# Memory attention: output products of the second token half run between the first half's scores, with their weights loaded once per half

## The chip, the cores and the metric

One Trainium2 chip; the program runs on one of its cores. The metric is the device time of one execution in microseconds (us), lower is better. The kernel before takes 2602.53 us, the median of 3 runs (2601.81 to 2604.06).

## The reference

One layer of a hybrid decoder for 512 prompt tokens and 32 sample tokens (8 sequences of 4), width 2048, everything in float32. Cut to what matters here:

```python
x = x + token_mixer(rmsnorm(x, norm_mix_w), ...)
# memory cross-attention: 4 heads of 128, 256 memory rows
q = rmsnorm(x) @ w_mq
s = einsum('blhd,bmhd->bhlm', q, mem_k) * 128 ** -0.5
o = einsum('bhlm,bmhd->blhd', softmax(s), mem_v)
x = x + o.reshape(B, L, 512) @ w_mo          # 512 x 2048
x = x + (silu(h @ w_gate) * (h @ w_up)) @ w_down   # h = rmsnorm(x)
```

Prompt tokens share one memory, whose keys and values were made earlier in the program; each sample sequence has a key and a value cache of its own (`cache_mem_k`, `cache_mem_v`, 512 KB per sequence each).

## The kernel before

Activations lie transposed: a tile holds 128 of the 2048 channels on its partitions and all 544 tokens along its free dimension. `X` is the residual, 16 such tiles in four groups. Float32 products are made of split operands: each operand is a rounded high part and a low part (`hi`, `lo`), and a product is three matmuls, high by high, high by low, low by high. For a weight, `load_part` (L117 to L134) loads 512 KB into `wraw`, ScalarE (ACT) casts it to `whi` (L131), VectorE (DVE) subtracts (`wlo`, L132). Three `wraw` buffers and two pairs of parts exist; the parts are made one ahead of their use (`parts_ahead`).

Work of TensorE (PE) that can fill gaps is put into a queue `line` of generators; `draw(n)` takes n matmuls (or small groups) from its head. The tile framework then orders the instructions of each engine by its own estimate of times, so the order in the program is not quite that of the source; each engine executes its order strictly.

The stage of this case lies between the mixer's output products and the SwiGLU:

- Eight query products (`add_mq`, 16 weight tiles of 3 matmuls each): four heads for tokens 256 to 543 (half 1), then four heads for tokens 0 to 255 (half 0).
- Between them, per head and half: scores (`x_scores`, `xs_ps`), a softmax on DVE and ACT, the turn of the probabilities on PE (`x_turn`, `xt_ps`), the products with the values (`x_values`, `xo_ps`), and the split of the result into `oxh` and `oxl` (`put_ox`).
- The samples' attention (`xsample`) in pieces: 16 pieces that turn keys and score them (`xk_ps`, `xss_ps`), a softmax, then eight pieces with the values (`xso_ps`). The 16 cache loads pass through three buffers (`xkv`), issued by SyncE's queue (SP), which executes its rows in order. `x_more` draws one piece. Half 1 of `ox` is complete only when the samples are done.
- The output products with `w_mo` (`add_mo(i, half)`, L1534 to L1567): for each of eight pairs of channel tiles (i) and each half of 272 tokens, 24 matmuls into `mo_ps`, of which there are two buffers. Then DVE adds the result to `X` (`x`, L1556), ACT squares it, and the squares are added up for the next norm, for half 0 on GpSimd (POOL, `SS`) and for half 1 on DVE (`SW`), both L1562. The weights of an i are loaded once and used for both halves.
- When both halves of an i are in `X`, `ffn_parts` (L1576 to L1595) makes operands of the SwiGLU's seven products (a Winograd scheme over halves of tokens and of channels): `B11` and `B21` from tokens 0 to 271 alone (ACT the high parts, DVE the low parts, L1583), and `b12`, `b22`, `t1`, `t2`, `t4` from both halves: ACT, DVE (`t`, L1534), POOL (`t`, L1589), DVE (`f`, L1534). The split of `t1` and `t2` into `T1` and `T2` (L606, L607) follows one i later. The SwiGLU's units (`unit`) use `B11`, `B21`, `T2`, `T1`, ... in this order; POOL combines weights for them (`scomb`, L1661) and operands (L1799).

The order of the output products is half 0 of i = 0 and 1 beside the last scores, then half 1 of i = 0 and 1, then for i = 2 to 7 half 1 and half 0.

Of the kernel before, what the change touches and what calls it, by code (L numbers as in the profile page):

```python
# [25 lines left out]
TT = TP + TS  # L26
# [18 lines left out]
def hybrid_step(ctx: ExitStack, tc: tile.TileContext, a):  # L45
    nc = tc.nc
    dma = nc.sync.dma_start
    dma2 = nc.gpsimd.dma_start
# [11 lines left out]
    dpool = pool("dpool", space=DRAM)  # L60
# [6 lines left out]
    def acc_tile(name):  # L67
        return ps_acc.tile([P, 2, 512], F32, tag="acc", name=name)
# [241 lines left out]
    line = deque()  # L310
# [3 lines left out]
    def parts_ahead(late=None):  # L314

        before = []
        for i in count():
            if i == late:
                yield from before
                before = []  # L320
            if not wants:
                break
            w, n0, k0, n, width = wants.popleft()
            now = [(k0 + j, *p) for j, p in enumerate(load_part(w, k0, n, n0, width))]
            yield from before
            before = now
        yield from before
# [295 lines left out]
    def xt(k):  # L623
        return X[k // 4][:, k % 4, :]
# [858 lines left out]
    def x_values(h, half):  # L1483
# [18 lines left out]

    for n, u in enumerate(units):
        need(("mq", *u))
        if n:
            x_turn(*units[n - 1])
            draw(4)
        else:
            draw(36)
        x_scores(*u)  # L1510
        draw(14)
        if n:
            x_values(*units[n - 1])
        for _ in range(6 if n >= MH - 1 else 0):
            x_more(1)
            draw(5)
    def ops_tiles(p, tag, name):
        return group(p, tag, name, F32R, (P, KH, HT))

    x3_d = dpool.tile([P, KD, TT], F32, name="x3_d")  # L1520
    h_d = dpool.tile([P, FF // P, TT], F32, name="h_d")
    fops = {}

    def x_ops(n, q):
        fops[q] = [ops_tiles(xnp, f"x{c}{n}", q + c) for c in "hl"]

    x_ops(0, "B11")
    x_ops(1, "B21")

    def ffn_w(out, o, t):  # L1530
        nc.scalar.activation(out, xt(o)[:, t], AF.Copy, scale=vcol("ffn", o))

    def ffn_w_less(out, o, t, y):
        nc.vector.scalar_tensor_tensor(out, xt(o)[:, t], vcol("ffn", o), y, ALU.mult, SPLIT)  # L1534

    S3 = [post.tile([P, 2, HT], F32, tag=t, name=t) for t in ("SS", "SW")]

    def add_mo(i, half, done=None):


        def run():
            if i not in mo_w:
                mo_w[i] = [next(wparts) for _ in range(MH)]
            acc = acc_tile("mo_ps")
            for k, hi, lo in mo_w[i]:
                xh, xl = ox[half][k]
                for u in range(2):
                    s = slice(u * P, (u + 1) * P)
                    for wt, xt_, at in ((hi, xh, 0), (hi, xl, 1), (lo, xh, 2)):
                        nc.tensor.matmul(  # L1550
                            acc[:, u, :HT], wt[:, s], xt_,
                            start=k + at == 0, stop=k == MH - 1 and at == 2,
                        )
                        yield
            x = X[i // 2][:, 2 * i % 4 : 2 * i % 4 + 2, (T0, T1)[half]]
            nc.vector.tensor_tensor(x, x, acc[:, :, :HT], ALU.add)  # L1556
            if i == 0:
                nc.scalar.activation(S3[half], x, AF.Square)
            else:
                t = post.tile([P, 2, HT], F32, tag="sqt", name="sqt", bufs=2)  # L1560
                nc.scalar.activation(t, x, AF.Square)
                (nc.vector if half else nc.gpsimd).tensor_add(S3[half], S3[half], t)  # L1562
            if done:
                done(i)

        line.append(run())


    mo_w, late, before = {}, [], []

    def t_parts(i, ts):
        for q, t in zip(("T1", "T2"), ts):
            split(*(t[:, i] for t in fops[q]), t)

    def ffn_parts(i):
        b12, b22, t4 = (t[:, i] for t in late)  # L1576
        ffn_w(b12, 2 * i, T1)
        ffn_w(b22, 2 * i + 1, T1)
        for u, q in enumerate(("B11", "B21")):
            o = 2 * i + u  # L1580
            hi, lo = (t[:, i] for t in fops[q])
            ffn_w(hi, o, T0)
            nc.vector.scalar_tensor_tensor(  # L1583
                lo, xt(o)[:, T0], vcol("ffn", o), hi.bitcast(F32), ALU.mult, SPLIT
            )
        t1 = ap.tile([P, HT], F32, tag="t1", name="t1", bufs=2)
        t2 = ap.tile([P, HT], F32, tag="t2", name="t2")
        ffn_w_less(t1, 2 * i, T0, b12)
        nc.gpsimd.tensor_tensor(t2, b22, t1, ALU.add)  # L1589
        ffn_w_less(t4, 2 * i + 1, T0, t2)  # L1590
        if before:
            t_parts(*before.pop())
        before.append((i, (t1, t2)))
        if i % 2:
            dma2(x3_d[:, 2 * i - 2 : 2 * i + 2], X[i // 2])  # L1595
# [516 lines left out]
```

## Time and profile before

| | |
|---|---|
| median of 3 runs | 2602.53 us |
| profiled execution | 2602.59 us, of it the span of its instructions 2600.8 us |
| PE busy | 2522.0 us, 97% of the span |
| DVE, ACT, POOL busy | 1687.6, 1583.4, 1079.2 us |
| query products (L1444) | 975.4 to 1063.0 us from the span's start |
| output products (L1550) | 1063.6 to 1133.0 us |

A row of the timeline names the engine, the line, the operation, output and inputs. Matmuls are pipelined: a row's own time (0.29 us) is longer than the distance to the next.

### The profile page before, as it was taken

Reading aid. Unit: us, or ns where it says so; the run is one execution under the profiler, and the core shown is the slowest. Engines: PE = TensorE matmul, PEld = TensorE weight load, DVE = VectorE, ACT = ScalarE, POOL = GpSimd, SP = SyncE. Lnnn points to the kernel's source line nnn. Section 1 sums busy time; section 2 is a strip of 40 time slices with the busy share of each in tenths; the row PEclk is TensorE's granted clock in tenths of the full one; section 3 lists DMA queues with packets and bytes.
Section 4 is the critical chain, followed back from the end, with each engine's and each line's share of the span. In section 5 each row is a group of like instructions: output and inputs, shape, how many; then the busy total and the mean of one; then the engine's idle time right before and its main releaser. Section 6 shows DMA issues by size and latency. Waiting matters only on the chain.

```text
span 2600.8 us, 48404 instructions
## 1 busy us (share of the span) xinstructions
PE 2522.0 (97%) x19679; PEld 2453.4 (94%) x19679; DVE 1687.6 (65%) x2575; ACT 1583.4 (61%) x2177; POOL 1079.2 (41%) x616
## 2 busy tenths in 40 slices
PE   8999999999999999989999999999999999999997
PEld 7999999998999998879999999999999999999997
DVE  5555555556568795697665656565666666767897
ACT  5343222333326785467777777777777778777757
POOL 4101222112124631255555555555555656665622
PEclk9999999999999999999999999999999999999999
DMA  7222332454523326522333333333333453333325
GB/s 236 83 69 82 91 91 91 143 155 137 179 66 128 106 72 192 193 100 96 123 114 111 115 106 115 106 115 106 115 107 120 158 187 132 115 115 135 112 70 162
DMA packets 287168, 315.48 MB, mean 121 GB/s; under 512 B 9508, under 2 KB 239220, under 8 KB 284097
## 3 DMA queue, kind: packets, MB, share of 16 engines
q1 hardware_dynamic: 273024, 264.80, 32.0%
q0 software_dynamic: 13920, 47.58, 5.5%
q8 instruction: 155, 2.54, 0.4%
q14 instruction: 69, 0.56, 0.1%
HBM read 278.28 MB, written 33.64 MB: 120 GB/s over the span
## 4 chain that ended last, share of the span: by engine, by line
PE 83%; DVE 7%; ACT 4%; issue 2%; DMA 2%; POOL 1%; SPq 0%; ACTq 0%; POOLq 0%; DVEq 0%
PE s_ps L1696 49%; PE in_ps L345 18%; PE o_ps L1149 4%; PE ha_ps L933 2%; PE d_ps L154 1%; DVE wlo L132 1%; PE mq_ps L1444 1%; PE o_ps L509 1%; PE s_ps L471 1%; DMA wraw<-in_w_in_dram 1%; DVE slo L1644 1%; PE mkv_ps L684 1%; PE in_ps L154 1%; DMA wraw<-in_w_down_dram 1%; PE t_ps L489 0%
## 5 line engine op out<-in xcount | busy, mean ns | idle before, releaser
L1644 DVE TENSOR_TENSOR slo<-scomb,h 128x1024 fp32r<-128x1024 f32 x256 | 311.5, 1217 | 132.3 <-PE s_ps L1696 113.9
L131 ACT CAST whi<-wraw 128x1024 fp32r<-128x1024 f32 (+1 forms) x204 | 169.7, 846 | 351.8 <-PE in_ps L345 278.0
L1642 ACT CAST h<-scomb 128x1024 fp32r<-128x1024 f32 x256 | 260.9, 1019 | 132.0 <-DVE slo L1644 118.7
L1661 POOL TENSOR_TENSOR scomb<-sraw 128x1024 f32<-128x1024 f32 x128 | 315.8, 2467 | 9.4 <-DVE slo L1644 4.4
L1643 ACT CAST shi<-scomb 128x1024 fp32r<-128x1024 f32 x256 | 269.7, 1053 | 53.0 <-PE s_ps L1696 49.5
L1661 POOL TENSOR_TENSOR scomb<-sraw,scomb 128x1024 f32<-128x1024 f32 x64 | 166.7, 2605 | 287.4 <-DVE slo L1644 241.6
L345 PE MATMUL in_ps<-xh,whi 128*128 128x272 f32 x1280 | 276.9, 297 | 0.8 <-ACT whi L131 0.8
L345 PE MATMUL in_ps<-xl,whi 128*128 128x272 f32 x1280 | 275.1, 295 | 0.0
L345 PE MATMUL in_ps<-xh,wlo 128*128 128x272 f32 x1280 | 272.9, 294 | 0.8 <-DVE wlo L132 0.8
L132 DVE TENSOR_TENSOR wlo<-wraw,whi 128x1024 fp32r<-128x1024 f32 (+1 forms) x204 | 208.3, 1034 | 98.8 <-ACT whi L131 94.8
L1696 PE MATMUL s_ps<-T,shi 128*128 128x272 f32 x1408 | 269.3, 288 | 2.8 <-ACT shi L1643 2.8
L1642 ACT CAST h<-sraw 128x1024 fp32r<-128x1024 f32 x192 | 195.3, 1017 | 122.3 <-DVE slo L1644 121.9
L611 DVE TENSOR_TENSOR gu<-gu,s_ps 128x272 f32<-128x272 f32 x264 | 111.6, 437 | 237.4 <-PE s_ps L1696 237.4
L1696 PE MATMUL s_ps<-dT,shi 128*128 128x272 f32 x1280 | 243.8, 289 | 0.0
L1644 DVE TENSOR_TENSOR slo<-sraw,h 128x1024 fp32r<-128x1024 f32 x192 | 233.2, 1215 | 10.7 <-ACT h L1642 7.3
L1643 ACT CAST shi<-sraw 128x1024 fp32r<-128x1024 f32 x192 | 201.5, 1049 | 56.5 <-PE s_ps L1696 48.0
L1696 PEld LDWEIGHTS s_ps<-T,shi 128*128 128x128 f32 x1408 | 221.2, 188 | 3.3 <-ACT shi L1643 3.0
L345 PEld LDWEIGHTS in_ps<-xh,wlo 128*128 128x128 f32 x1280 | 202.6, 189 | 6.4 <-issue 4.4
L345 PEld LDWEIGHTS in_ps<-xh,whi 128*128 128x128 f32 x1280 | 202.2, 189 | 6.7 <-issue 4.3
L345 PEld LDWEIGHTS in_ps<-xl,whi 128*128 128x128 f32 x1280 | 202.5, 189 | 5.1 <-issue 4.4
L1696 PE MATMUL s_ps<-T,slo 128*128 128x272 f32 x704 | 203.6, 289 | 1.2 <-DVE slo L1644 1.2
L1696 PEld LDWEIGHTS s_ps<-dT,shi 128*128 128x128 f32 x1280 | 201.1, 188 | 0.0
(521 smaller groups left out, 7371.6 us busy)
## 6 DMA issues: line engine op xcount, KB each, us to landing
sraw<-in_w_gate_dram SPq DMA_DIRECT2D x44, 1024.0 KB, 5.3
sraw<-in_w_up_dram SPq DMA_DIRECT2D x44, 1024.0 KB, 5.3
wraw<-in_w_in_dram SPq DMA_DIRECT2D x84, 512.0 KB, 4.0
sraw<-in_w_down_dram SPq DMA_DIRECT2D x40, 1024.0 KB, 5.3
oraw<-in_w_out_dram SPq DMA_DIRECT2D x32, 512.0 KB, 3.9
h_d<-gu POOLq DMA_DIRECT2D x22, 544.0 KB, 3.9
wraw<-in_w_mk_dram SPq DMA_DIRECT2D x16, 512.0 KB, 3.7
wraw<-in_w_mv_dram SPq DMA_DIRECT2D x16, 512.0 KB, 3.8
```

The source lines that it names most:

```text
L131: nc.scalar.copy(hi[:, s], raw[:, s])
L132: nc.vector.tensor_tensor(lo[:, s], raw[:, s], hi[:, s].bitcast(F32), SPLIT)
L154: nc.tensor.matmul(acc[:, i, : e - b], wt, xt[:, b:e], start=first, stop=last)
L345: nc.tensor.matmul(acc[:, i, : e - b], wt, xt[:, b:e], start=j + at == 0, stop=j == KD - 1 and at == 2,)
L611: nc.vector.tensor_tensor(out, x, y, ALU.add)
L933: nc.tensor.matmul(pairs(pa[:, b], hb), kp[:, c], odd(qq[:, c], hb), start=True, stop=True)
L1149: nc.tensor.matmul(acc[:, p, :HT], wt[:, k, s], xt_[:, k], start=first and k + at == 0, stop=k == DN - 1 and at == 2, skip_group_check=True,)
L1642: first = nc.scalar.copy(h2, src)
L1643: nc.scalar.copy(hi, src)
L1644: return first, nc.vector.tensor_tensor(lo, src, h2.bitcast(F32), SPLIT)
L1661: return t, nc.gpsimd.tensor_tensor(t, x, y, op)
L1696: nc.tensor.matmul(accs[p], wt[:, k, s], xt_[:, k], start=k + at == 0, stop=k == n - 1 and at == 2,)
```

## The change

The output products are queued right behind the query products, all eight i of half 1 first. Half 1's are drawn while the last scores of half 0 run, and to the end; only then come all eight i of half 0. Each product takes its own weight parts, so `w_mo` is loaded and split 16 times instead of 8. For this the samples' attention moves forward: 14 pieces after each of the fourth and fifth scores (with what is left right after the fifth), instead of 6 after each of the last five. Since half 1 is now the half that is ready first, the names swap: `T0` (from which `B11` and `B21` are made) is tokens 272 to 543, `T1` tokens 0 to 271. `ffn_parts` is cut in two: `first_parts` (`B11`, `B21`) runs behind each half 1 product, `other_parts` (the rest) behind each half 0 product.

```diff
+    T0, T1 = slice(HT, TT), slice(0, HT)
...
+    def add_mo(i, half, done):
+
+        wants.append((w_mo, 2 * i * P, 0, MH, 2 * P))
+
+        def run():
+            if half and i == 0:
+                x_ops(0, "B11")
+                x_ops(1, "B21")
+            acc = acc_tile("mo_ps")
+            for _ in range(MH):
+                k, hi, lo = next(wparts)
+                xh, xl = ox[half][k]
...
+            x = X[i // 2][:, 2 * i % 4 : 2 * i % 4 + 2, slice(*HALF[half])]
...
+            done(i)
...
+    def first_parts(i):
+        for u, q in enumerate(("B11", "B21")):
...
+    def other_parts(i):
+        b12, b22, t4 = (t[:, i] for t in late)
...
     for u in units:
         add_mq(*u)
+    for half, done in ((1, first_parts), (0, other_parts)):
+        for i in range(KH):
+            add_mo(i, half, done)
+    rest = [line.pop() for _ in range(KH)][::-1]
     pieces = xsample(qs)
...
-        for _ in range(6 if n >= MH - 1 else 0):
+        for _ in range(14 if n in (MH - 1, MH) else 0):
             x_more(1)
             draw(5)
...
-            if i not in mo_w:
-                mo_w[i] = [next(wparts) for _ in range(MH)]
...
+        if n == MH:
+            x_more(100)
     x_turn(*units[-1])
-    x_more(2)
+    draw(24)
     x_values(*units[-1])
-    add_mo(0, 0)
-    add_mo(1, 0)
-    while len(line) > 0 or next(pieces, 0) is None:
+    while line:
         draw(4)
-        x_more(1)
...
-    add_mo(0, 1, ffn_parts)
-    add_mo(1, 1, ffn_parts)
-    for i in range(2, KH):
-        add_mo(i, 1)
-        add_mo(i, 0, ffn_parts)
     x_ops(2, "T1")
     x_ops(3, "T2")
+    line.extend(rest)
     while line:
         draw(1)
```

The order of DVE before, around i = 3 and 4 of the output products (`x_...` is a group of the residual, `t_...` and `f_...` are `t1`/`t2` and `b12`, `b22`, `t4`):

```order
L1534 SCALAR_TENSOR_TENSOR t_11927<-x_10201,vec_403,f_11676 128x272
L132 TENSOR_TENSOR wlo<-wraw,whi 128x1024
L1583 SCALAR_TENSOR_TENSOR B11l<-x_10201,vec_403,B11h 128x272
L1583 SCALAR_TENSOR_TENSOR B21l<-x_10201,vec_403,B21h 128x272
L1556 TENSOR_TENSOR x_8499<-x_8499,mo_ps 128x2x272
L607 TENSOR_TENSOR T1l<-t_11927,T1h 128x272
L1562 TENSOR_TENSOR SW<-SW,sqt 128x544
L1534 SCALAR_TENSOR_TENSOR f_11678<-x_10201,vec_403,t_11928 128x272
L607 TENSOR_TENSOR T2l<-t_11928,T2h 128x272
L1556 TENSOR_TENSOR x_8499<-x_8499,mo_ps 128x2x272
```

The order of DVE in the change where half 1 ends (i = 7) and half 0 begins:

```order
L1534 TENSOR_TENSOR x_8848<-x_8848,mo_ps 128x2x272
L132 TENSOR_TENSOR wlo<-wraw,whi 128x1024
L1540 TENSOR_TENSOR SW<-SW,sqt 128x544
L1558 SCALAR_TENSOR_TENSOR B11l<-x_8848,vec_403,B11h 128x272
L1558 SCALAR_TENSOR_TENSOR B21l<-x_8848,vec_403,B21h 128x272
L1534 TENSOR_TENSOR x_9922<-x_9922,mo_ps 128x2x272
L132 TENSOR_TENSOR wlo<-wraw,whi 128x1024
L1534 TENSOR_TENSOR x_9922<-x_9922,mo_ps 128x2x272
L1509 SCALAR_TENSOR_TENSOR t_11972<-x_9922,vec_403,f_11924 128x272
L132 TENSOR_TENSOR wlo<-wraw,whi 128x1024
```

What stood mixed per i now stands in two stretches: eight times the first five rows for half 1, and behind them for half 0 the additions to `x`, `t`, `f`, `T1l`, `T2l` and six `wlo`. POOL's rows (`SS`, `t`, `scomb`, L1799) are the same as before in nearly the same order, but all of them stand behind the second stretch's first rows.

The order of SP in the change, from the samples' last key load to the output weights:

```order
L1349 DMA xkv<-in_cache_mem_v_dram 128x2x512
L123 DMA wraw<-in_w_mo_dram 128x4x256
L1349 DMA xkv<-in_cache_mem_v_dram 128x2x512
L123 DMA wraw<-in_w_mo_dram 128x4x256 x2
L1349 DMA xkv<-in_cache_mem_v_dram 128x2x512 x5
L123 DMA wraw<-in_w_mo_dram 128x4x256 x4
```

The five last value loads still stand in one piece; behind them come 13 loads of `w_mo` where there were five.

## Rows read from the trace of the kernel before

**Rows 1.** The page, busy time and share of the span of PE
```profile
PE 2522.0 (97%) x19679; PEld 2453.4 (94%) x19679; DVE 1687.6 (65%) x2575; ACT 1583.4 (61%) x2177; POOL 1079.2 (41%) x616
```

**Rows 2.** Windows of the stage: length, busy of PE, PEld, DVE, ACT, POOL, clock, DMA
```profile
1024.00:1063.50 39.50, 38.72 (x392) 31.93 (x391) 15.46 (x33) 19.00 (x40) 4.84 (x6) 1.00 0.61 191
1063.50:1078.00 14.50, 12.97 (x127) 9.84 (x126) 5.12 (x14) 4.38 (x13) 1.69 (x3) 1.00 0.54 174
1078.00:1145.00 67.00, 54.16 (x392) 51.74 (x390) 63.34 (x81) 42.55 (x80) 33.47 (x24) 0.95 0.39 137
```

**Rows 3.** Windows of 2 us, same columns
```profile
1114.00:1116.00 2.00, 2.00 (x11) 2.00 (x10) 2.00 (x2) 0.00 (x0) 2.00 (x2) 0.50 0.00 0
```

**Rows 4.** Timeline of DVE: start, us, operation, idle before
```profile
1078.30 1.35 DVE L1556 TENSOR_TENSOR x<-x,mo_ps 128x544 f32<-128x544 f32 x2 [0.98 <-PE mo_ps L1550]
...
1082.34 0.49 DVE L1583 SCALAR_TENSOR_TENSOR B11l<-x,vec,B11h 128x272 fp32r<-128x272 f32 x1
...
1105.08 0.71 DVE L1556 TENSOR_TENSOR x<-x,mo_ps 128x544 f32<-128x544 f32 x1
1105.71 1.99 DVE L607 TENSOR_TENSOR T1l<-t,T1h 128x272 fp32r<-128x272 f32 x1
1107.62 3.03 DVE L1562 TENSOR_TENSOR SW<-SW,sqt 128x544 f32<-128x544 f32 x1
...
1144.14 0.43 DVE L607 TENSOR_TENSOR T2l<-t,T2h 128x272 fp32r<-128x272 f32 x1
```

**Rows 5.** Timeline of POOL
```profile
1104.82 2.57 POOL L1661 TENSOR_TENSOR scomb<-sraw 128x1024 f32<-128x1024 f32 x1
1107.36 2.72 POOL L1799 TENSOR_TENSOR f<-f,f 128x1088 f32<-128x1088 f32 x1
...
1130.87 1.36 POOL L1562 TENSOR_TENSOR SS<-SS,sqt 128x544 f32<-128x544 f32 x1 [3.23 <-ACT sqt L1561]
1133.49 0.76 POOL L1589 TENSOR_TENSOR t<-f,t 128x272 f32<-128x272 f32 x1 [1.27 <-DVE t L1534]
```

**Rows 6.** Groups of DVE, 1078 to 1145 us: count, busy, mean ns, idle before
```profile
L1556 DVE TENSOR_TENSOR x<-x,mo_ps 128x544 f32<-128x544 f32 x16 | 11.3, 712 | 1.0 <-PE mo_ps L1550 1.0
L1583 DVE SCALAR_TENSOR_TENSOR B11l<-x,vec,B11h 128x272 fp32r<-128x272 f32 x8 | 9.3, 1168 | 0.7 <-ACT B11h L1531 0.5
...
L132 DVE TENSOR_TENSOR wlo<-wraw,whi 128x1024 fp32r<-128x1024 f32 x6 | 7.3, 1219 | 0.3 <-ACT whi L131 0.3
L1534 DVE SCALAR_TENSOR_TENSOR f<-x,vec,t 128x272 f32<-128x272 f32 x8 | 4.0, 496 | 1.2 <-POOL t L1589 1.2
...
L607 DVE TENSOR_TENSOR T2l<-t,T2h 128x272 fp32r<-128x272 f32 x8 | 3.5, 433 | 0.0
L1644 DVE TENSOR_TENSOR slo<-sraw,h 128x1024 fp32r<-128x1024 f32 x2 | 2.4, 1211 | 0.0
```

**Rows 7.** Groups of POOL, 1078 to 1145 us, same columns
```profile
L1562 POOL TENSOR_TENSOR SS<-SS,sqt 128x544 f32<-128x544 f32 x7 | 11.0, 1578 | 18.6 <-ACT sqt L1561 18.4
L1589 POOL TENSOR_TENSOR t<-f,t 128x272 f32<-128x272 f32 x8 | 7.5, 933 | 13.1 <-DVE t L1534 10.1 <-DVE T2l L607 3.0
L1799 POOL TENSOR_TENSOR f<-f,f 128x1088 f32<-128x1088 f32 x2 | 5.3, 2626 | 0.0
L1661 POOL TENSOR_TENSOR scomb<-sraw 128x1024 f32<-128x1024 f32 x2 | 5.1, 2570 | 0.0
L1661 POOL TENSOR_TENSOR scomb<-scomb,sraw 128x1024 f32<-128x1024 f32 x1 | 2.6, 2574 | 0.0
```

**Rows 8.** A window of 10 us, columns as in the group of windows above
```profile
1080.00:1090.00 10.00, 10.00 (x81) 9.94 (x80) 8.69 (x14) 8.67 (x17) 2.69 (x3) 1.00 0.79 264
```

**Rows 9.** Groups of PE, 1024 to 1145 us (20 matmul rows are five units)
```profile
L1486 PE MATMUL xo_ps<-pT,vm__10511 128*128 128x256 f32 x20 | 5.2, 384 | 0.1
...
L1475 PE MATMUL xt_ps<-ident,p 128*128 128x128 f32 x20 | 3.1, 279 | 0.1
```

**Rows 10.** DMA issues, 1015 to 1075 us: count, KB each, us to landing
```profile
xkv<-in_cache_mem_v_dram SPq DMA_DIRECT2D x8, 512.0 KB, 4.7
```

More of the change, by code (lines that the diff above doesn't have):

```diff
@@ L1491, in x_values, with ops_tiles, x_ops, ffn_w @@
         put_ox(h, slice(b0, b0 + 2 * P), po[:, : 2 * P])
+    T0, T1 = slice(HT, TT), slice(0, HT)
+    def ops_tiles(p, tag, name):
+        return group(p, tag, name, F32R, (P, KH, HT))
+    x3_d = dpool.tile([P, KD, TT], F32, name="x3_d")
+    h_d = dpool.tile([P, FF // P, TT], F32, name="h_d")
+    fops = {}
+    def x_ops(n, q):
+        fops[q] = [ops_tiles(xnp, f"x{c}{n}", q + c) for c in "hl"]
+    def ffn_w(out, o, t):
+        nc.scalar.activation(out, xt(o)[:, t], AF.Copy, scale=vcol("ffn", o))
@@ new lines, in ffn_w_less @@
+    def ffn_w_less(out, o, t, y):
+        nc.vector.scalar_tensor_tensor(out, xt(o)[:, t], vcol("ffn", o), y, ALU.mult, SPLIT)
+    S3 = [post.tile([P, 2, HT], F32, tag=t, name=t) for t in ("SS", "SW")]
+    def add_mo(i, half, done):
[8 more added lines that the diff above has]
+                xh, xl = ox[half][k]
+                for u in range(2):
+                    s = slice(u * P, (u + 1) * P)
+                    for wt, xt_, at in ((hi, xh, 0), (hi, xl, 1), (lo, xh, 2)):
+                        nc.tensor.matmul(
+                            acc[:, u, :HT], wt[:, s], xt_,
+                            start=k + at == 0, stop=k == MH - 1 and at == 2,
+                        )
+                        yield
+            x = X[i // 2][:, 2 * i % 4 : 2 * i % 4 + 2, slice(*HALF[half])]
+            nc.vector.tensor_tensor(x, x, acc[:, :, :HT], ALU.add)
+            if i == 0:
+                nc.scalar.activation(S3[half], x, AF.Square)
+            else:
+                t = post.tile([P, 2, HT], F32, tag="sqt", name="sqt", bufs=2)
+                nc.scalar.activation(t, x, AF.Square)
+                (nc.vector if half else nc.gpsimd).tensor_add(S3[half], S3[half], t)
+            done(i)
+        line.append(run())
@@ new lines, in hybrid_step, with t_parts @@
+    late, before = [], []
+    def t_parts(i, ts):
+        for q, t in zip(("T1", "T2"), ts):
+            split(*(t[:, i] for t in fops[q]), t)
+    def first_parts(i):
+        for u, q in enumerate(("B11", "B21")):
+            o = 2 * i + u
+            hi, lo = (t[:, i] for t in fops[q])
+            ffn_w(hi, o, T0)
+            nc.vector.scalar_tensor_tensor(
+                lo, xt(o)[:, T0], vcol("ffn", o), hi.bitcast(F32), ALU.mult, SPLIT
+            )
+    def other_parts(i):
+        b12, b22, t4 = (t[:, i] for t in late)
+        ffn_w(b12, 2 * i, T1)
+        ffn_w(b22, 2 * i + 1, T1)
+        t1 = ap.tile([P, HT], F32, tag="t1", name="t1", bufs=2)
+        t2 = ap.tile([P, HT], F32, tag="t2", name="t2")
+        ffn_w_less(t1, 2 * i, T0, b12)
+        nc.gpsimd.tensor_tensor(t2, b22, t1, ALU.add)
+        ffn_w_less(t4, 2 * i + 1, T0, t2)
+        if before:
+            t_parts(*before.pop())
+        before.append((i, (t1, t2)))
+        if i % 2:
+            dma2(x3_d[:, 2 * i - 2 : 2 * i + 2], X[i // 2])
@@ L1513, in hybrid_step @@
             x_values(*units[n - 1])
-        for _ in range(6 if n >= MH - 1 else 0):
+        for _ in range(14 if n in (MH - 1, MH) else 0):
             x_more(1)
             draw(5)
[L1517 to L1541, printed above, removed]
-            if i not in mo_w:
-                mo_w[i] = [next(wparts) for _ in range(MH)]
[L1544 to L1566, printed above, removed]
@@ L1569, in hybrid_step @@
[L1569 to L1595, printed above, removed]
@@ L1597, in hybrid_step @@
-    for i in range(KH):
-        wants.append((w_mo, 2 * i * P, 0, MH, 2 * P))
-    wparts = parts_ahead(late=2)
+        if n == MH:
+            x_more(100)
     x_turn(*units[-1])
-    x_more(2)
+    draw(24)
     x_values(*units[-1])
-    add_mo(0, 0)
-    add_mo(1, 0)
-    while len(line) > 0 or next(pieces, 0) is None:
+    while line:
         draw(4)
-        x_more(1)
     xa_ctx.close()
```

## The prediction

> **What bounds the kernel now.** I read the page first: PE is busy 97% of the span [rows 1], so a change away from PE can give back only the few stretches where PE starves. The windows of the stage show one. From 1024 to 1063.5 us PE is busy nearly throughout and DVE for 15.5 of 39.5 us; from 1078 to 1145 us DVE is busy for 63.3 of 67 us and PE executes 392 matmuls [rows 2]. A full stretch of PE has 81 in 10 us, 0.123 us each [rows 8]; with 0.125 us, the distance of two such matmuls, 392 take 49 us, so PE loses 18 us there. DVE paces it: PE waits for the addition to `x` that frees an accumulator.
>
> But DVE is not slow by its own work alone. Its rows overlap the next by 0.08 us (the `x` row at 1105.08 lasts 0.71 us, the next begins 0.63 us later), so I take 0.08 us off each: 0.63 `x`, 0.41 `B11l` when it runs free (the row at 1082.34), 1.14 `wlo`, 0.41 `t` or `f`, 0.35 `T2l`, 1.13 `slo` [rows 4, 6]. Yet `T1l`, with the shape of `T2l`, lasts 1.99 us at 1105.71 and ends just after POOL's `scomb` of 1104.82 does, and `SW`, with the shape of `x`, lasts 3.03 us and ends 0.6 us after POOL's L1799 [rows 4, 5]. `x` at 1105.08 ran at full speed inside the same `scomb`; it reads PSUM. So **an operation of DVE that reads two SBUF tensors and an operation of POOL take turns**, and the stretch is bounded by the sum of both.
>
> The sum bears it out. POOL from 1078 to 1145: 7 `SS`, 8 `t`, 2 L1799, 3 `scomb` [rows 7], by free lengths 1.33, 0.73, 2.6 and 2.54 us [rows 5, 7], 27.9 us. DVE's operations with two SBUF tensors: 16 `B11l` or `B21l` (6.6), 16 `t` or `f` (6.6), 16 `T1l` or `T2l` (5.6), 7 `SW` (4.4), 6 `wlo` (6.8), 30.0 us. Together 57.9 us of the 66.3 between the first `x` (1078.3) and the last `T2l` (1144.6) [rows 4]. The other 8.4 us is what shows of DVE's operations that read PSUM, 16 `x` and 4 `slo`, 14.6 us: 0.575 of them. The last `T2l` is what the SwiGLU's third product waits for, so that is where this stage ends for PE.
>
> The Trainium skill ("SBUF — State Buffer", section "SBUF: two separate sides") states this as an exclusive lock between GpSimd and a VectorE operation with two SBUF inputs, the loser blocking for the whole instruction. The rows named agree, 1.99 and 3.03 us where 0.35 and 0.63 are free. By that rule the time is a sum of both engines, without it the larger of the two, which is the second rival below.
>
> **The change, part by part.**
>
> *Matmuls.* The same 384 for the output products, and the same attention: PE gains no work.
>
> *Weights loaded twice.* Eight more loads of 512 KB, eight more casts on ACT (1 us each, in a stretch where ACT is busy 42.6 of 67 us [rows 2]) and eight more `wlo`, 9.1 us of DVE. Six `wlo` stand in the half 0 stretch as in the stretch before; the others stand beside half 1, where POOL has nothing to do. The loads: each i is 24 matmuls, 3 us of PE or more, for 512 KB, and the DMA share is 0.39 [rows 2]; I cost them at nothing. Without that cover a load's 4.7 us [rows 10] would show against 3 us of products, 1.7 us an i.
>
> *The samples' attention moved forward.* It is the same PE work, with fewer query products between the last pieces. SP's five last value loads stand in one piece, each waiting for one of three buffers; a load takes 4.7 us to land [rows 10], so the last two cannot be there until about 5 us after the fourth and fifth pieces were consumed. I take 1.5 us of wait for them, and 1.2 us for the turn and split of the samples' result, which half 1's first product now waits for and where before products of half 0 ran. Counting the groups of PE by program order, half 1's first output matmul comes at about 1066 us, where the first one was at 1063.6. Bounds: 1062 (nothing waits) and 1070 (each of the last four loads adds 1.5 us).
>
> *Half 1's stretch.* PE from 1066: 192 matmuls at 0.125, 24.0 us; four turns and four value products left, by their groups 0.6 and 1.0 us each [rows 9], 6.4 us, less 0.4 for what runs under other rows: 30 us, 1096. DVE per i has `x` 0.63, `wlo` 1.14, `SW` 0.63, `B11l` and `B21l` 0.82: 3.2 us against PE's 3.0, with POOL idle. Six i behind the last scores lose 0.2 us each, 1.2; the last softmax, with little beside it, 1.2; and behind the last `x` of half 1 `wlo`, `SW`, `B11l`, `B21l` (2.6 us) come before half 0's first `x`. That `x` begins at about 1101 us. Bounds: 1096.6 (PE without a gap) and 1106 (a later start and a wait for each of the last softmaxes).
>
> This moves 11.0 us of DVE's two-tensor work (the `B` rows and `SW`) out of the contended stretch. That is the gain.
>
> *Half 0's stretch.* All of POOL's 27.9 us stays: `SS` belongs to half 0, `t` needs both halves, and the combinations stand behind them on POOL's queue. DVE's two-tensor work is 6 `wlo` (6.8), 16 `t` or `f` (6.6), 16 `T` (5.6): 19.0. Together 46.9 us, plus 0.575 of 8 `x` and 4 `slo` (9.5), 5.5: 52 us to the last `T2l`. PE has only 30 us of work there (24 of products, 6 of the SwiGLU's `B11` and `B21`), so it starves for some 20 us. Bounds: 46.9 (all PSUM reads hidden) and 54.
>
> *Sum.* 1101 + 52 = 1153 against 1144.6: **+8.4 us**. Before, POOL's 27.9 us began at 1080; now they begin after 1101, because the half on which they hang comes last, while POOL idles beside half 1. The 11.0 us that leave the stretch, and the 3.3 us of shown PSUM reads with them, do not pay for a start 22.7 us later. What follows (the operand splits, the norm, the units) is unchanged.
>
> *The clock.* Where PE idled around 1110 us the granted clock fell to half (0.50 at 1114, 11 matmuls in 2 us [rows 3]), that is 1.2 GHz. In half 0's stretch it will fall again, but there DVE and POOL set the pace, and it costs little; it would cost 3 us if it held through the 24 matmuls behind the last `T2l`, and as before it probably holds through some of them. I count the two cases as equal.
>
> Profiled execution: 2602.59 + 8.4 = 2611.0 us; the median of the runs, 2602.53, stands 0.06 below it, so 2611.0 stays. That is 0.32% slower; a measurement of this kernel tells 0.2%, some 5 us, from no change.
>
> **The rivals.**
>
> 1. *Half 1 runs without a gap and the turn-taking hides every PSUM read.* Then half 0 begins at 1096.6 and takes 46.9 us: 1143.5, 1 us earlier than before, 2601.5 us. For it: DVE was idle 60% of the time from 1024 to 1063.5, so there is room for half 1's work. Against it: 0.575 of the PSUM reads did show. Cases in between, up to +5 us, count here. Chance 0.26.
>
> 2. *Faster: the longer engine counts, not the sum.* If POOL's and DVE's operations mostly fall beside each other in half 0, because fewer two-tensor operations of DVE are in the queue and its waits for POOL's `t` coincide with POOL's other work, the stretch takes DVE's own 28.5 us, and PE's 30 decides: 1101 + 30 + 1 for the last `T2l`, 1132, 12.6 us earlier, 2590. The point from which it decides: less than half of POOL's 27.9 us blocking DVE. For it: before, POOL sat idle for half of the stretch (33.5 busy of 67 [rows 2]). Against it: the eight `B11l` alone lasted 9.3 us where 3.9 are free [rows 4, 6], so POOL did block DVE. Chance 0.12, with what lies between it and -5 us.
>
> 3. *The loads do show.* If half 0's weights, queued behind one another on SP and with only three buffers, come late at each i, 1.7 us for eight i add up to 13 us on PE, of which the 20 us of starving swallow most; beside half 1 nothing swallows them. I take +5 on the forecast: 2616. For it: 13 loads in a row on SP. Against it: a DMA share of 0.39. Part of the forecast's side; chance 0.08.
>
> That the change does not do what it says can be excluded: the order of DVE and SP shows both stretches and the extra loads.
>
> **How the numbers follow.** The forecast, +5 to +15 us, has 0.54, the third rival 0.08, so slower 0.62; the first rival 0.26, no change; the second 0.12, faster. The predicted time is the forecast's, 2611. Range: the earliest start and shortest stretch give 2601.5, and a little of what lies below is taken in, 2599; the latest start and the longest stretch, 1106 + 54 = 1160, give +15.4, 2618.
>
> **What would show it.** Right: half 1's `B11l` rows all near 0.49 us, POOL empty until about 1103 us, then DVE rows of 1 to 3 us again, `T1l` and `f` above all, the last `T2l` near 1153, PE short of matmuls between 1105 and 1150. Wrong: half 0's stretch clearly under 45 us, or DVE's two-tensor rows there at their free length; a first output matmul after 1070 would put the loss into the samples' loads instead.

## The result, and the profile after

The changed kernel takes 2621.43 us (median of 6 runs, 2614.55 to 2622.81), the kernel before 2601.96 us (6 runs, 2599.21 to 2604.06). The ratio is 1.0071, 95% interval 1.006 to 1.0082: slower by 19.5 us. Slower was forecast, but 8.4 us of it, and 2621 lies outside the range that ended at 2618. The profiled execution of the changed kernel is its slowest run, 2622.81 us (span 2621.0). All medians here are of undisturbed executions: e4 and e6 below each leave out one far slower run, so that e6 stands at 2611.96 us where the expectations of e16 and e17 reckon with 2613.2.

The windows of the stage, to set against [rows 2, 3, 8] (us, then busy time and count of PE, weight load, DVE, ACT, POOL; granted clock; DMA share; GB/s):

```profile
1065.00:1070.00 5.00, 1.66 (x45) 0.91 (x38) 2.49 (x4) 0.00 (x0) 1.69 (x1) 1.00 0.80 275
1070.00:1075.00 5.00, 5.00 (x26) 4.62 (x27) 0.77 (x4) 1.51 (x6) 0.00 (x0) 0.66 0.12 37
...
1105.00:1110.00 5.00, 5.00 (x41) 4.82 (x40) 5.00 (x10) 3.46 (x6) 0.00 (x0) 1.00 0.55 171
...
1120.00:1125.00 5.00, 0.66 (x4) 0.30 (x2) 5.00 (x6) 3.15 (x6) 2.66 (x4) 0.98 0.51 207
1125.00:1130.00 5.00, 4.54 (x20) 4.54 (x21) 5.00 (x5) 2.22 (x5) 4.08 (x2) 0.50 0.07 30
```

PE starves twice: at 1065, ahead of the first output product, and from 1120 on, in half 0's stretch. Behind either gap the granted clock is low, and a window holds 20 or 26 matmuls where 41 fit. In between, half 1's stretch fills PE.

The first gap, on PE's timeline (start, length, operation, idle time before and what ended it):

```profile
1068.89 0.64 PE L1414 MATMUL xso_ps<-xkv,xpm 128*32 128x128 f32 x16 [2.75 <-DMA xkv<-in_cache_mem_v_dram]
1069.94 0.33 PE L1424 MATMUL xot_ps<-ident,xos 128*128 128x128 f32 x1 [0.40 <-DVE xos L1422]
...
1070.54 0.73 PE L1528 MATMUL mo_ps<-oxh,whi 128*128 128x272 f32 x1
```

The last value tile of the samples comes 2.75 us late, and the first output product follows it at 1070.54. Then DVE and POOL, which answer to [rows 4, 5]:

```profile
1080.30 0.49 DVE L1558 SCALAR_TENSOR_TENSOR B11l<-x,vec,B11h 128x272 fp32r<-128x272 f32 x1
...
1109.09 0.72 DVE L1534 TENSOR_TENSOR x<-x,mo_ps 128x544 f32<-128x544 f32 x1
...
1121.99 3.42 DVE L132 TENSOR_TENSOR wlo<-wraw,whi 128x1024 fp32r<-128x1024 f32 x1
...
1132.51 2.62 DVE L1509 SCALAR_TENSOR_TENSOR f<-x,vec,t 128x272 f32<-128x272 f32 x1
...
1138.95 0.71 DVE L1534 TENSOR_TENSOR x<-x,mo_ps 128x544 f32<-128x544 f32 x1
...
1143.04 2.77 DVE L607 TENSOR_TENSOR T2l<-t,T2h 128x272 fp32r<-128x272 f32 x1
...
1156.96 0.43 DVE L607 TENSOR_TENSOR T2l<-t,T2h 128x272 fp32r<-128x272 f32 x1
```

```profile
1111.87 0.60 POOL L1575 DMA_DIRECT2D x_d<-x  x1 [44.70 <-DVE x L1534]
1112.49 1.66 POOL L1569 TENSOR_TENSOR t<-f,t 128x272 f32<-128x272 f32 x1
...
1132.43 2.40 POOL L1661 TENSOR_TENSOR scomb<-scomb,sraw 128x1024 f32<-128x1024 f32 x1
...
1138.69 2.58 POOL L1661 TENSOR_TENSOR scomb<-sraw 128x1024 f32<-128x1024 f32 x1
...
1151.43 2.69 POOL L1799 TENSOR_TENSOR f<-f,f 128x1088 f32<-128x1088 f32 x1
...
1254.75 0.60 POOL L1844 DMA_DIRECT2D h_d<-gu  x1 [5.26 <-DVE gu L1843]
```

POOL is idle for 44.7 us beside half 1, and DVE's rows have their free lengths there; from 1112 us both work, and rows of 0.35 to 1.2 us last 2 to 3. `f` at 1132.51, with two SBUF tensors, waits beside POOL's `scomb`; `x` at 1138.95, which reads PSUM, has its free length inside the next one. The last `T2l` ends at 1157.4, 12.8 us later than before. The second store of the feed-forward block's product (`h_d`, at 1254.75) is 18.2 us later than in the kernel before:

```profile
1236.59 0.59 POOL L1844 DMA_DIRECT2D h_d<-gu  x1 [6.08 <-DVE gu L1843]
```

From there PE is busy without a gap until the down products. So 5.4 us go between the last `T2l` and that store, where the forecast had nothing, and 2.0 us after it, at two places near 2100 and 2490 us where PE stands in both kernels (granted clock 0.93 and 0.87 over 25 us there, 1.00 and 0.93 before); no run shows why.

### The profile page after: what moved, and what is told of

Read it like the earlier page. It is cut to its first block, busy times and chain, and to the rows that moved or that the text cites. A ratio compares the mean times of both kernels' runs of the same rounds, so it can differ in the third digit from the quotient of the medians.

```text
span 2621.0 us, 48444 instructions
## 1 busy us (share of the span) xinstructions
PE 2533.2 (97%) x19679; PEld 2462.9 (94%) x19679; DVE 1699.8 (65%) x2583; ACT 1592.1 (61%) x2185; POOL 1081.1 (41%) x616
## 4 chain that ended last, share of the span: by engine, by line
PE 52%; DVE 3%; ACT 2%; POOL 1%; issue 1%; DMA 1%; ACTq 0%; DVEq 0%; POOLq 0%
PE s_ps L1696 49%; PE d_ps L154 1%; PE mo_ps L1528 1%; DVE slo L1644 1%; ACT shi L1643 1%; POOL scomb L1661 0%; ACT h L1642 0%; DMA wraw<-in_w_down_dram 0%; DVE wlo L132 0%; PE y_ps L1958 0%; DMA xkv<-in_cache_mem_v_dram 0%; POOL SS L1540 0%; DVE hl L607 0%; DMA hB<-h_d 0%; PE mq_ps L1444 0%
## 5 line engine op out<-in xcount | busy, mean ns | idle before, releaser
L131 ACT CAST whi<-wraw 128x1024 fp32r<-128x1024 f32 (+1 forms) x212 | 178.0, 853 | 357.5 <-PE in_ps L345 279.6
L132 DVE TENSOR_TENSOR wlo<-wraw,whi 128x1024 fp32r<-128x1024 f32 (+1 forms) x212 | 221.5, 1057 | 109.0 <-ACT whi L131 106.3
```

Source lines behind the costliest of these rows:

```text
L131: nc.scalar.copy(hi[:, s], raw[:, s])
L132: nc.vector.tensor_tensor(lo[:, s], raw[:, s], hi[:, s].bitcast(F32), SPLIT)
```

## The experiments

The table puts every run beside two marks of its own trace: the end of the last `T2l` and the start of the second `h_d` store, both counted from the first query product, since the stage itself starts 1 to 5 us earlier or later from run to run. I take a mark of a single profiled execution as good to some 2 us: the samples' first key turn comes 39.7 to 41.9 us after the first query product in these traces, and 43.5 us in the changed kernel's. The ratios are to the kernel before on the same chip, whose medians were 2601.3 to 2602.0.

| run | median us | ratio to before, 95% | last T2l | second h_d |
|---|---|---|---|---|
| before | 2601.96 | | 169.2 | 261.2 |
| changed | 2621.43 | 1.006 to 1.0082 | 182.2 | 279.6 |
| e2 changed, sums swapped | 2619.75 | 1.006 to 1.0085 | 178.6 | 275.9 |
| e5 changed, f behind t | 2618.01 | 1.0051 to 1.0079 | 179.4 | 275.9 |
| e7 changed, splits by PSUM | 2616.40 | 1.0042 to 1.0067 | 175.3 | 273.1 |
| e10 changed, norm later | 2613.84 | 1.0027 to 1.0055 | 179.2 | 270.8 |
| e6 changed, half the values | 2611.96 | 1.0025 to 1.0053 | 175.2 | 270.2 |
| e14 = e5, e7, e10 | 2610.20 | 1.002 to 1.0044 | 173.6 | 271.8 |
| e15 = e14, e2 | 2613.20 | 1.0032 to 1.0059 | 176.2 | 269.0 |
| e17 = e6, e10 | 2606.65 | 1.0006 to 1.0024 | 173.3 | 265.0 |
| e4 before, sums on DVE | 2605.35 | 1.001 to 1.0034 | 166.6 | 263.5 |
| e8 before, splits by PSUM | 2600.72 | 0.9984 to 1.0002 | 168.2 | 259.9 |
| e11 before, norm later | 2604.18 | 0.9995 to 1.0013 | 169.6 | 262.7 |
| e12 = e4, e11 | 2604.28 | 1.0001 to 1.0018 | 166.7 | 263.5 |
| e13 = e12, e8 | 2599.03 | 0.9981 to 1.0001 | 165.8 | 259.3 |
| e16 before, half the values | 2599.43 | 0.9979 to 0.9997 | 166.5 | 257.9 |
| e18 before, pieces gathered | 2608.82 | 1.0018 to 1.0042 | 176.4 | 267.9 |

### Do DVE and POOL take turns, and what is a turn worth?

e2 and e4, the running sums of squares on the other engine (e4 is the kernel before with `nc.vector` alone):

```diff
-                (nc.vector if half else nc.gpsimd).tensor_add(S3[half], S3[half], t)
+                (nc.gpsimd if half else nc.vector).tensor_add(S3[half], S3[half], t)
```

> The changed kernel with one word moved: the running sum of squares of the first half (tokens 272 to 543) on POOL, which is idle there, and that of the second half on DVE. Turn-taking (DVE operations that read two SBUF tensors and POOL operations exclude each other): in the second half's stretch POOL loses 7 sums of 1.33 us or more (9.3 us) and DVE gains 7 of 0.71 us (5.0 us), so the stretch from its first x add to the last T2l falls from 48.3 to about 44 us and the time from 2621.4 to about 2617. Own-count rival (each engine pays only its own operations; DVE is busy throughout that stretch): DVE has 5.0 us more, so about 2626. TensorE rival (the stretch is set by the product order, not by DVE and POOL): within 1 us of 2621.

> The kernel before with both halves' running sums of squares on DVE, none on POOL. Turn-taking: POOL loses 7 sums of 1.37 us or more (9.6 us), DVE gains 7 of 0.71 us (5.0 us), both in the stretch from 1078 to 1145 us: about 4.6 us less, 2597. Own-count rival: DVE is busy in nearly all of that stretch, 5.0 us more, 2607. TensorE rival: 2602 within 1 us.

None of the theories has its numbers: e2 is 1.7 us under the changed kernel, within its interval, and e4 4.0 us over the kernel before. That is nearest to the own-count rival, but e4's last `T2l` is 2.6 us earlier, not later; 4.9 us are lost behind it. The rows show the turns. The groups of DVE in half 1's stretch, first of the changed kernel, then of e2 (count, busy us, mean ns of one):

```profile
L1558 DVE SCALAR_TENSOR_TENSOR B11l<-x,vec,B11h 128x272 fp32r<-128x272 f32 x8 | 4.0, 495 | 0.0
L1558 DVE SCALAR_TENSOR_TENSOR B21l<-x,vec,B21h 128x272 fp32r<-128x272 f32 x8 | 4.0, 495 | 0.0
```

```profile
L1558 DVE SCALAR_TENSOR_TENSOR B11l<-x,vec,B11h 128x272 fp32r<-128x272 f32 x8 | 10.8, 1348 | 0.5 <-ACT B11h L1506 0.2
...
L1558 DVE SCALAR_TENSOR_TENSOR B21l<-x,vec,B21h 128x272 fp32r<-128x272 f32 x8 | 3.9, 490 | 0.0
```

With no POOL work `B11l` takes 495 ns; with seven sums on POOL it takes 1348. (`B21l` and `x` keep their lengths in e2, but no POOL row stands beside them there.) I then took every DVE row's length beyond its kind's free one and summed it: 0.2 us in half 1's stretch of the changed kernel (POOL 0), 6.9 us there in e2 (POOL busy 10.7 us), 17.9 us in the changed kernel's half 0 stretch (POOL 35.6), 18.1 us in the stretch before (POOL 33.5 [rows 2]). **Half to two thirds of POOL's busy time shows as DVE's waiting**, not all of it. Of the rest, a part is POOL's own waiting (its `t` at 1112.49 lasts 1.66 us, where 0.76 is free [rows 5]), a part falls beside DVE's PSUM reads; how much each is stays open. The half 0 stretch is 48.3 us in the changed kernel and 45.9 in e2: 7.3 us less waiting, 5.0 more of DVE's own sums. Half 1 pays most of it back: half 0's first `x` comes 132.7 us after the first query product in e2, 129.9 to 130.8 in e5, e7, e10 and e14, which leave that part as in the changed kernel.

e7 and e8, the splits of the output weights through a PSUM copy (the PSUM pool is opened ahead of the last products for it):

```diff
+        if by_psum and width == 2 * P:
+            by_psum[0](*(t[:, :m].rearrange("p (k c) -> p k c", c=width) for t in (hi, lo, raw)))
+            return [(hi[:, s], lo[:, s]) for s in cs]
...
+    by_psum.append(split_w2)
```

> The changed kernel with the second pass's eight weight splits reading their high part from a PSUM copy (one more ACT copy of 1.02 us each), as the SwiGLU units' splits do, whose rows are 1.21 us whatever POOL does. Turn-taking: the wlo rows of 3.42, 2.37 and 1.77 us fall to 1.2 us each (3.9 us in sum), TensorE's waits for wlo (3.47 and 3.08 us) mostly go, the stretch falls by about 4 us: 2617. Own-count rival: DVE's count is unchanged and ACT has 8.2 us more, so 2621 or slower.

> The kernel before with the output products' weight splits through PSUM, as in e7_wlo_psum. By that run (5.0 us less on the changed kernel) taking DVE's two-SBUF operations out of POOL's way is worth their blocked excess: the stretch from the first x add to the last T2l falls from 66.3 to 62 us, and the time to about 2598. Rival (what e4_before_sums_dve showed: any reordering of the output products loses about 4 us behind the last T2l, since the order of the gate product's splits changes with it): stretch shorter by 4, time within 1 us of 2602.

The groups of DVE in half 0's stretch, of the changed kernel and of e7:

```profile
L132 DVE TENSOR_TENSOR wlo<-wraw,whi 128x1024 fp32r<-128x1024 f32 x6 | 11.2, 1870 | 0.3 <-ACT whi L131 0.3
L607 DVE TENSOR_TENSOR T2l<-t,T2h 128x272 fp32r<-128x272 f32 x8 | 8.1, 1009 | 0.0
...
L1509 DVE SCALAR_TENSOR_TENSOR f<-x,vec,t 128x272 f32<-128x272 f32 x8 | 7.4, 920 | 0.7 <-POOL t L1569 0.7
```

```profile
L1514 DVE SCALAR_TENSOR_TENSOR f<-x,vec,t 128x272 f32<-128x272 f32 x8 | 10.2, 1271 | 1.9 <-POOL t L1574 1.9
...
L1635 DVE TENSOR_TENSOR wlo<-wraw,h 128x1024 fp32r<-128x1024 f32 x6 | 7.3, 1212 | 0.0
...
L612 DVE TENSOR_TENSOR T2l<-t,T2h 128x272 fp32r<-128x272 f32 x8 | 3.4, 430 | 0.0
```

The splits come free of POOL, as expected, and the stretch falls from 48.3 to 44.7 us. But part of POOL's turns falls on other rows with two SBUF tensors instead: `f` goes from 920 to 1271 ns and `t` from 692 to 934, while `T2l` falls to its free length. PE's wait for `wlo` did not go, against the expectation: it is 6.6 us in e7 and 6.5 in the changed kernel. The time is 5.0 us less, with intervals that just overlap. In e8 the same edit gave 0.9 us of stretch and no difference in time.

### Is POOL's `f` ahead of the last `t` the wait behind the output products?

```diff
-        nc.gpsimd.tensor_tensor(t2, b22, t1, ALU.add)
+        t_last[:] = [nc.gpsimd.tensor_tensor(t2, b22, t1, ALU.add)]
...
+            with tc.issue_after(t_last[0].ins):
+                for s in (slice(0, 4), slice(4, 8)):
+                    nc.gpsimd.tensor_tensor(late[0][:, s], late[0][:, s], late[1][:, s], SPLIT)
```

> The changed kernel with both subtractions f = f - f on POOL (128x1088, 2.7 us each, which nothing needs until the T3 operand) held behind the last t of the output products. In the changed kernel the last one runs from 1151.4 to 1154.1 ahead of the last t, ACT's T2h waits 2.96 us for that t with the weight split of the gate product behind it on ACT, and TensorE stands 4.24 us and comes back at half clock. If this place is a part of the loss behind the last T2l: last T2l 2.7 us earlier, and up to 2 us more from the clock, so 2617 to 2619. If the subtractions only move the same turn to the gate product behind it: 2621 within 1 us.

2618.0 us, as forecast for the first theory, but the interval is also that of the changed kernel, and the trace decides against it: half 0's stretch is 48.7 us, not shorter, and PE's wait of 4.24 us for ACT's `shi` is replaced by 3.60 us for a weight split on DVE and 1.7 us for `shi`. The edit moved the block: POOL's two `f` now run from 1148.5 to 1153.6 us, behind the last `t`, and DVE's last `f` and `T2l` beside them take 2.70 and 1.60 us.

### What is lost behind the last `T2l`?

```diff
         def first_gate(i):
-            if i == 2:
+            if i == 4:
                 norm_rows(R3, S3, "s")
```

> The changed kernel with the norm rows of the feed-forward block (five DVE operations for each half, of which those beside POOL's scomb take 2.3 to 2.5 us) issued behind the fourth weight split of the up product in place of the second, so that no weight split of it stands behind them. If the loss behind the last T2l (97.35 us to the second h_d store against 92.0 before) is this order on DVE: TensorE's wait of 3.6 us for slo and its half clock behind it go, 92 to 93 us, time about 2617. If the backlog of DVE and POOL is what counts, the wait turns up in front of the gate's multiplication or of the next split: 97 us, 2621.

> The kernel before with the same move of the norm rows; its order of DVE instructions there is then the same as in e10_after_norm4. If the order is what counts: TensorE's waits of 2.83 and 1.48 us there go, 2598, and the difference between this pair is about 5 us smaller than between the changed kernel and the kernel before (19.5 us). If the backlog counts: 2602, and the pair differs by 19 to 20 us.

PE's waits from the last `T2l` to the second `h_d` store (us in total, times, longest), of the kernel before, of the changed kernel, then of e10:

```profile
PE s_ps L1696 <- ACT shi L1643: 2.8, 1, 2.8
PE s_ps L1696 <- DVE slo L1644: 2.4, 3, 1.5
PE s_ps L1696 <- ACT gu L1717: 2.2, 1, 2.2
```

```profile
PE s_ps L1696 <- DVE slo L1644: 7.2, 6, 3.6
...
PE s_ps L1696 <- DVE T L607: 0.3, 1, 0.3
```

```profile
PE s_ps L1696 <- DVE slo L1644: 2.0, 5, 0.8
PE s_ps L1696 <- ACT shi L1643: 0.8, 1, 0.8
```

e10 takes 91.7 us from the last `T2l` to that store, the changed kernel 97.4, the kernel before 92.0; the time falls by 7.6 us, more than expected. (The wait of 4.24 us for `shi` ends 0.6 us ahead of the last `T2l`, and e10 has one of 4.25 at the same place: it is no part of this.) So the loss behind is the order on DVE, where the norm rows stand ahead of a weight split that PE needs at once. In the changed kernel's DVE timeline two of them are blocked, and the split behind them ends PE's wait of 3.6 us:

```profile
1189.05 2.30 DVE L87 SCALAR_TENSOR_TENSOR nt<-nt,nv 128x272 f32<-128x272 f32 x1
1191.38 2.48 DVE L88 SCALAR_TENSOR_TENSOR R<-nt,R 128x272 f32<-128x272 f32 x1
1193.78 0.43 DVE L1234 TENSOR_SCALAR nv<-nr_ps 128x272 f32<-128x272 f32 x1
1194.13 1.20 DVE L1644 TENSOR_TENSOR slo<-scomb,h 128x1024 fp32r<-128x1024 f32 x1
```

The kernel before has blocked norm rows ahead of splits too:

```profile
1173.36 2.46 DVE L86 TENSOR_TENSOR nt<-R 128x272 f32<-128x272 f32 x1 [0.41 <-ACT R L85]
1175.86 2.51 DVE L87 SCALAR_TENSOR_TENSOR nt<-nt,nv 128x272 f32<-128x272 f32 x1
...
1179.45 1.22 DVE L1644 TENSOR_TENSOR slo<-scomb,h 128x1024 fp32r<-128x1024 f32 x1
```

There they cost PE less: waits of 2.83 and 1.48 us at a granted clock of 1.00, against 3.60, 1.68 and 0.40 us in the changed kernel, with the clock at 0.83 over the 10 us behind the longest. Counted from matmul starts more than 0.126 us apart, from 30 us behind the last `T2l` to the second store, PE loses 10.2 us in the changed kernel (9.7 to 11.2 in e2, e4, e5, e6 and e7, which have its order there), 5.3 in the kernel before (5.1 to 5.3 in e8, e16 and e18) and 6.1 to 6.7 in every run with the later norm. The same move gives the kernel before nothing (e11: 93.1 us behind the last `T2l`, time within the interval). And the order by halves is not what makes that order: e4, which only moves the sums, has the changed kernel's order of DVE around the norm rows, and 96.9 us behind its last `T2l`.

### Do the samples' loads cost it, and because they are gathered?

e6 and e16 load four of the samples' eight value tiles and use each for two samples, so they leave out half of these loads and the samples' outputs are other numbers; e18, the second edit below, is the kernel before with the changed kernel's gathering:

```diff
-        later = [(ck, b) for b in range(2, DB)] + [(cv, b) for b in range(DB)]
+        later = [(ck, b) for b in range(2, DB)] + [(cv, b) for b in range(0, DB, 2)]
...
-            if later:
+            if later and b % 2 == 0:
...
-            vs = kvs.popleft()
+            vs = kvs.popleft() if b % 2 == 0 else vs
```

```diff
-        for _ in range(6 if n >= MH - 1 else 0):
+        for _ in range(14 if n in (MH - 1, MH) else 0):
```

> The changed kernel with four of the samples' eight value tiles loaded (each used for two samples; the samples' outputs are other numbers). If the gathered samples' pieces are bound by their loads: the wait of 2.75 us for the last value tile and the fall of the granted clock behind it (half clock from 1070 to 1073.5 us) go, the first output product comes 3 to 5 us earlier after the first key turn (51.9 us behind it in the changed kernel), and 2621.4 becomes about 2617. If the pieces' own order sets it (POOL's masks, TensorE's small matmuls): first output product within 1 us, 2621.

> The kernel before with four of the samples' eight value tiles loaded, as in e6_half_values (control; the samples' outputs are other numbers). There e6_half_values was 8.2 us under the changed kernel. If the loads cost because the change gathers the pieces: at most the 1.1 us that TensorE waits for value tiles in the kernel before, 2600.5 to 2602. If eight value loads cost any order of the work as much: 2596 or less.

> The kernel before with the changed kernel's gathering of the samples' 28 pieces alone: 14 in each of two units of queries, in place of 6 in each of the last five. Its queue of loads is then that of the changed kernel up to the output products. If gathering makes the loads bind: TensorE waits 2 to 4 us for value tiles and the time is 2604 to 2607. If the loads bind only because the output products stand right behind the pieces (here the second half's query products still run): within 1 us of 2602.

e6 is 9.5 us under the changed kernel, and its first output product follows the first key turn after 47.3 us where the changed kernel takes 51.9. The control e16 gains 2.5 us, so some 7 us are the loads in the changed kernel. The gathering alone (e18) costs the kernel before 6.9 us: its PE waits of that stage, then its windows, then those of the kernel before:

```profile
PE xso_ps L1414 <- DMA xkv<-in_cache_mem_v_dram: 2.5, 1, 2.5
...
PE xt_ps L1475 <- DVE oxl L1338: 1.4, 1, 1.4
PE xso_ps L1414 <- POOL xpm L1405: 1.4, 2, 1.1
```

```profile
1060.00:1070.00 10.00, 5.53 (x63) 3.55 (x64) 5.34 (x14) 2.04 (x7) 2.42 (x2) 0.84 0.64 207
1070.00:1080.00 10.00, 9.03 (x38) 7.02 (x37) 2.61 (x9) 4.84 (x15) 0.00 (x0) 0.65 0.01 2
```

```profile
1060.00:1070.00 10.00, 9.44 (x118) 6.94 (x110) 3.72 (x8) 2.82 (x7) 3.29 (x5) 1.00 0.86 286
1070.00:1080.00 10.00, 8.62 (x68) 7.21 (x69) 2.83 (x8) 2.65 (x8) 0.00 (x0) 1.00 0.44 141
```

With the pieces gathered PE is left without other products, waits for a tile and for POOL's masks, and runs the next 10 us at a granted clock of 0.65, with 38 matmuls where the kernel before has 68.

### Do the parts add up, and does a version beat both?

> The changed kernel with four value tiles loaded and the norm rows behind the fourth split (e6_half_values and e10_after_norm4 together). If the two losses lie at different places: 8.2 and 7.6 us off 2621.4, about 2606, and what is left to the kernel before is some 4 us. If a stage that starts earlier only has the same backlog behind it (as the three edits of e14 that gave 11.2 of 16 us): 2609 or more.

> The changed kernel with the three single edits together (f behind the last t, weight splits through PSUM, norm rows behind the fourth split). If they act at different places their measured gains of 3.4, 5.0 and 7.6 us add up: 2605.4. If the first two relieve the same wait ahead of the last T2l: 2608 to 2609. In both cases the order by halves stays behind the kernel before (2602).

> As e14_after_f_psum_norm4, with the sums swapped as in e2_sums_swapped (2.4 us off the second half's stretch there, of which POOL's slower sums in the first half took some back). Turn-taking: 2 us less than e14_after_f_psum_norm4. Own-count rival: within 1 us of it or slower, since DVE then has 5 us more in the stretch that it fills.

> The kernel before with both sums on DVE (e4_before_sums_dve) and the norm rows behind the fourth split (e11_before_norm4). In e4_before_sums_dve the last T2l came 2.6 us earlier after the first query product than in the kernel before, and 4.9 us went behind it; in e10_after_norm4 the moved norm rows brought that loss back. If the loss behind is the order on DVE alone: 92 us to the second h_d store again, 2598 to 2600. If it is DVE's and POOL's backlog: 96 us or more, 2603 to 2606.

> As e12_before_dve_norm4, with the weight splits through PSUM as well. Turn-taking: with the sums gone from POOL and the splits out of its way the stretch from the first x add to the last T2l falls from 65.6 to about 62 us, 2595 to 2597. If the stretch of the kernel before is held by TensorE's products and x adds in its first half (e8_before_wlo_psum: 0.9 us of 4): 1 us less than e12_before_dve_norm4.

e17 lies 14.8 us under the changed kernel, where the two edits alone sum to 17.1, each good to some 3 or 4 us: those losses are at different places and add, within that. What is left of it over its control e16 is 7.2 us of time and 6.8 us at the last `T2l`, with the same 91 to 92 us behind it.

The edits ahead of the last `T2l` don't add to the one behind. e14 has its `T2l` 5.6 us earlier than e10 and its second store 1.0 us later; the time, 3.6 us under e10's, is within their overlapping intervals. The windows from 3 us behind the last `T2l`, of e14, then of e10:

```profile
1150.00:1160.00 10.00, 8.39 (x55) 8.17 (x54) 7.56 (x6) 6.00 (x7) 6.30 (x3) 0.83 0.13 44
1160.00:1170.00 10.00, 8.10 (x52) 7.67 (x51) 9.08 (x10) 6.38 (x7) 4.19 (x2) 0.86 0.21 65
```

```profile
1160.00:1170.00 10.00, 9.97 (x74) 9.75 (x74) 8.95 (x10) 7.63 (x9) 8.09 (x3) 0.94 0.12 38
1170.00:1180.00 10.00, 9.67 (x72) 8.96 (x71) 6.39 (x9) 7.00 (x9) 1.80 (x1) 1.00 0.67 210
```

In e14 PE comes to operand and weight splits that are not ready, waits, and the clock falls: 107 matmuls in 20 us against 146, 39 x 0.125 = 4.9 us given back. e12 has the backlog's number, 96.8 us behind its `T2l`: moving the norm rows brought e4 nothing in sum, and the second store stands at 263.5 in both. In e12 PE loses 3.5 us less than in e4 at the norm rows and 2.9 us more in the first 30 us behind the last `T2l`. So the order of the norm rows is the loss of the changed kernel; it is not the only thing that can stand there. e15 misses turn-taking's number: half 0's stretch is 44.7 us against e14's 43.7, and the time is 3.0 us above e14's, within overlapping intervals. e13 lies 5.3 us under e12 with a stretch 2.7 us shorter, neither of its two numbers. No version with all its loads beats the kernel before: e13's 2599.03 us has an interval that reaches 1.

## Why the prediction was wrong, step by step

**Right: slower, and the order by halves behind it.** POOL idles beside half 1 and starts late. With the two other losses taken out (e17 against e16) the last `T2l` is 6.8 us later, where the sum said 8.4. Its two parts were each off in the changed kernel, and the errors partly cancel by luck: half 0 began 8.1 us late and ran 3.7 us short. That POOL's late start is what makes the 6.8 us is argued from the rows; no run moves it alone, and e2, which starts POOL in half 1, gains nothing clear.

**Half 0's stretch, 52 us: 48.3, inside its bounds.** The turns are real, but the sum counted every microsecond of POOL against DVE; half to two thirds show. The factor of 0.575 for PSUM reads was fitted to one stretch and hid that. (The sum's own terms, 46.9 and 5.5, make 52.4, and the 3.3 us of shown PSUM reads are 2.9 by its factor.) The Trainium skill ("SBUF — State Buffer", section "SBUF: two separate sides") calls the SBUF port that GpSimd and VectorE share an exclusive lock. `B11l` at 1348 ns in e2, and `x` at 0.71 us inside a `scomb` of the changed kernel, agree with who blocks whom. What it costs a stretch was half to two thirds of POOL's time here. The Trainium skill ("Perfetto Trace Analysis", section "Optimizing Scalar/DVE Operations") warns that offloading between these two engines might not help. e4 agrees: 0.7 us of stretch for seven sums moved, and no gain in time.

**Failed: half 0's first `x` at 1101, at most 1106. It came at 1109.1.** The mis-sized term is "the samples' attention moved forward", 1.5 us of waiting and 1.2 us of split. The prediction's own test for it was a first output product after 1070: it came at 1070.5. PE waited 2.9 us for value tiles, 1.4 us for POOL's masks (1.1 and 0.5 in the kernel before) and 0.4 us for the turn's operand, and the half clock that followed took 15 matmuls out of the next 5 us (26 of 41), 1.9 us. I had counted the clock as equal in both kernels and had not priced a gap ahead of half 1. e18 sets the gathering at 6.9 us. Another 2.5 us belong to the profiled execution alone, whose first key turn comes late. Counted from the first query product, the forecast had half 0's first `x` at 125.6 us and at most 130.6; it came at 133.9 here, at 129.9 to 130.8 in e5, e7, e10 and e14, and at 125.0 in e17, with half the loads. From the first output product to that `x` 38.6 us went where the forecast had 35; 1.9 of the difference is the half clock, the other 1.7 stays open.

**Failed: "what follows is unchanged".** 5.4 us to the second store and 2.0 us later, against 0. I took the last `T2l` as the point behind which both kernels are the same program. They are, but not in the same order: DVE's instructions behind it are ordered otherwise, and at the norm rows PE loses 10.2 us where it lost 5.3. e10 gave 7.6 us back. The 2.0 us stay open. The forecast followed the order of DVE to the last `T2l` and no further.

**Right: the weights loaded twice cost nothing.** In half 1's stretch PE waits 1.0 us for `wlo` and `whi` in all, and in half 0's none of ACT's waits is for a load of them. That is read from the waits; no run loads them once in this order. The third rival's 5 us did not come from there, though it named the queue of loads. The first rival falls with the gap, though half 0's 48.3 us are nearer to its 46.9 than to the forecast's 52; the second falls with 46.9 us of busy DVE in 48.3.

So of 19.5 us, some 7 are the gathering (e18, measured in the kernel before; e6 less its control agrees), 5.7 (at the second store) to 7.6 (in time, e10) the order of the norm rows, and 4.5 to 7 what is left for the order by halves itself: e17 less its control is 7.2 us, and 4.5 if e11's 2.7 us for the later norm, which its interval does not tell from nothing, is taken into the control.

## What to carry to other kernels

When the rows of two engines take turns, find out what share of the one's busy time shows as the other's waiting before summing them; here it was half to two thirds. Work pulled together to clear the way leaves its own latency bare: the samples' loads had been hidden by being spread among query products. And a stage that is "the same behind" is so only if its instruction order is: an edit upstream can change how a scheduler orders what follows (e4 did it by moving one running sum), so compare the orders until both kernels run without a gap.

## What the runs showed of the hardware

Gains at one place were taken back by the clock at the next: PE that arrives earlier at operands that are not ready waits, and is granted 0.83 to 0.86 over the next 20 us (e14) where 0.94 and 1.00 stand without the gain (e10). Taking one operation of DVE out of POOL's way moved a part of the block to others (e7: `wlo` 1870 to 1212 ns, `f` 920 to 1271). In the changed kernel `x`, which reads PSUM, kept its 0.71 us inside a POOL row of 2.58, where `f`, with two SBUF tensors, took 2.62 beside one of 2.40.
